# A scratch slot held longer, and the block sums of one weight chunk in eight moved from GpSimd to VectorE, in a two-layer encoder

## The chip, the cores and the metric

The kernel runs on one core of a Trainium2 chip. The metric is the device time of one execution in microseconds (us). A core has five engines that run side by side and wait for each other through semaphores: TensorE (PE, matmuls; PEld is its weight load), VectorE (DVE), ScalarE (ACT), GpSimd (POOL) and SyncE (SP, which here only issues DMAs). Each engine takes its own instructions strictly in order: one that waits holds up all that stand behind it on that engine.

## The reference, cut to what matters

A trunk of two pre-norm residual layers over 512 tokens of width 1024. Layer 0 mixes with two kinds of attention heads, layer 1 with a neighbourhood attention whose scores get a learned relative position bias. After each mixing step comes a squared-ReLU MLP of width 4096, and a norm ends the whole:

```python
def sq_relu_mlp(h, w_up, w_down):
    u = jax.nn.relu(h @ w_up)
    return (u * u) @ w_down
...
        h = h + sq_relu_mlp(rmsnorm(h, norm_ffn[layer]), ffn_w_up[layer], ffn_w_down[layer])
    return rmsnorm(h, final_norm)
```

Everything is float32. The bias of layer 1 is `rpb[:, rblk, cblk]`, looked up for each query and key in its window.

## The kernel before, in words

**Precision.** Every float32 operand of a matmul is split into a high half, rounded to the matmul's format (`F32R`), and a low half, the rest. ACT makes the high half by a copy, DVE (sometimes POOL) the low half by a subtraction. A product is three matmuls: high by high, high by low, low by high (`mm3`, L604 to L606; L448 to L450 for blocks of 256 columns).

**Memory.** Large tiles live in 32 slots of 128 x 1024 (`Slot`). `take` takes the first of the list `free`, `give` appends to its end, at the time the program is built. A new tile of a slot waits, on the chip, until the last reader of the slot's tile before is done. Weight chunks pass through `wp`: four `raw` buffers (loaded by SP), three `whi`, four `wlo`.

**Weights.** `plan` writes down which chunks will be needed, `weights(i)` brings chunk `i` up and looks ahead: up to five loads, two splits. Three kinds of chunk matter here. `chunk` loads and splits. `summed_chunk` (L245 to L260) lets ACT write `wlo` as the negated raw chunk (L255), then a DMA on POOL's queue adds the weights from memory onto it (L256), and ACT writes `whi` (L259). `seven_chunk` (L349 to L367) loads two blocks of 128 rows by 256 columns, forms the four further block sums by three POOL instructions (L356, L357, L358; 128, 256 and 128 wide), then has ACT write `whi` (L362) and DVE `wlo` (L363), seven blocks of 128 columns each.

**Seven blocks.** `Seven` multiplies 2 x 2 blocks with seven block products instead of eight. `sums` and `split` bring the other factor into seven blocks, each a high and a low half, in slots of its own (DVE L390, L393, L418, L422 and ACT L417 where `convert` does it). `run` multiplies: for each of its weight chunks 7 x 3 matmuls of 256 columns (L448 to L450), then ACT and DVE put the result together (L456 to L460).

**The MLP.** `mlp(l, last)` is called once per layer, `last` only in the second. Its second half goes like this. `product8` multiplies eight hidden tiles `U` by eight chunks of the down weights into all eight PSUM banks: the first two chunks interleaved, then chunk by chunk, and the last two (U6, U7) output column by output column, each column being added to the residual `hT` by DVE (L1536). Beside it `convert` turns the other hidden tiles, in pairs `R` (eight pairs in the first MLP, seven in the second), into the seven blocks, and in the first MLP `bias_rows` builds the bias tables of layer 1: it loads the bias in pieces into one slot (`R` there), POOL spreads it over another (`F`, L1481 to L1484), and SP writes 32 pieces of `F` to the DRAM tile `bx` (L1490, L1495). Then `F` is given back. During this part `reserve` forbids weight chunks to take slots. Next `u7.run` goes over four groups `m` of 256 output columns, with eight (seven) weight chunks in each; each group's result is added to `hT` (L1574). In the first group of the first MLP `beside` also splits the last pair `V` into two tiles `U4` (`split`: high half L964 on ACT, low half L961 on DVE), which a last plain product multiplies after the groups (`gens4`).

**Order.** A scheduler puts the instructions of each engine in order when the program is built. What is wrapped in `tc.keep_in_program_order` (`held`) keeps its place; so do the block sums on POOL.

Of the kernel before, what the change touches and what calls it, by code (L numbers as in the profile page):

```python
# [12 lines left out]
ALU = mybir.AluOpType  # L13
# [5 lines left out]
P = 128  # L19
# [11 lines left out]
def f32(ap):  # L31
    return ap.bitcast(F32)
# [3 lines left out]
def encoder_kernel(ctx: ExitStack, tc: tile.TileContext, ins, out, dbg=None):  # L36
    nc = tc.nc
    PE, ACT, DVE, POOL, SP = nc.tensor, nc.scalar, nc.vector, nc.gpsimd, nc.sync
# [22 lines left out]
    def nm(s):  # L61
        cnt[0] += 1
        return f"{s}_{cnt[0]}"
# [198 lines left out]
    def rows(w, k0, nk):  # L262
        return w[k0 * P : (k0 + nk) * P, :].rearrange("(k p) n -> p k n", p=P)
# [6 lines left out]
    def plan(*spec, make=None):  # L270
        asked.append((make or chunk, spec))
        return len(asked) - 1
# [71 lines left out]

    reserve = [3]

    def seven_chunk(w, k0, c0):


        slot = Slot(F32) if len(free) > reserve[0] else None  # L350
        raw = slot.t if slot else wp.tile([P, 1024], F32, tag="raw", bufs=4, name=nm("raw"))
        SP.dma_start(raw[:, 0:512].rearrange("p (k n) -> p k n", k=2), rows(w, k0, 2)[:, :, c0 : c0 + 256])
        r = raw.rearrange("p (b n) -> p b n", n=P)
        yield
        held = tc.keep_in_program_order
        held(POOL.tensor_tensor(r[:, 6], r[:, 0], r[:, 1], op=ALU.subtract))  # L356
        held(POOL.tensor_tensor(r[:, 4:6], r[:, 2:3].to_broadcast([P, 2, P]), r[:, 0:7:6], op=ALU.add))  # L357
        held(POOL.tensor_tensor(r[:, 7], r[:, 3], r[:, 5], op=ALU.subtract))  # L358
        yield
        hi = wp.tile([P, 1024], F32R, tag="whi", name=nm("whi"))  # L360
        lo = wp.tile([P, 1024], F32R, tag="wlo", bufs=4, name=nm("wlo"))
        ACT.activation(hi[:, 0:896], raw[:, 128:1024], AF.Copy)  # L362
        DVE.tensor_tensor(lo[:, 0:896], raw[:, 128:1024], f32(hi[:, 0:896]), op=ALU.subtract)  # L363
        if slot:
            slot.free()
        yield hi, lo, []

    class Seven:
# [29 lines left out]
        def split(self, kp, held=lambda z: z):  # L398

            for b in range(7):  # L400
                i = self.number(kp, b) // 2
                if i not in self.slots:
                    self.slots[i] = Slot()
            raw, t = self.raw.pop(kp)
            own = isinstance(t, Slot)
            r, t_ = (s_.rearrange("p (b n) -> p b n", n=256) for s_ in (raw.t, t.t if own else t))

            T4 = t_[:, 2:3] if own else r[:, 3:4]
            src = lambda b, n: (r[:, 1 + b : 1 + b + n] if b < 3 else t_[:, b - 3 : b - 3 + n] if b < 5
                                else r[:, 0:1] if b == 5 else T4)  # L410
            b = 0
            while b < 7:
                q = self.number(kp, b)
                n = 2 if b == 3 or (b < 2 and q % 2 == 0) or (b == 5 and not own) else 1
                d = self.slots[q // 2].t.rearrange("p (q z n) -> p q z n", q=2, z=2)[:, q % 2 : q % 2 + n]
                s_ = r[:, 0:4:3] if b == 5 and n == 2 else src(b, n)
                ACT.activation(d[:, :, 0], s_, AF.Copy)  # L417
                held(DVE.tensor_tensor(d[:, :, 1], s_, f32(d[:, :, 0]), op=ALU.subtract))  # L418
                b += n
                yield  # L420
                if b == 3 and not own:
                    held(DVE.tensor_tensor(r[:, 3], r[:, 3], r[:, 0], op=ALU.subtract))  # L422
                    yield
            raw.free()
            if own:
                t.free()
# [4 lines left out]

        def plan(self, w, c0, pairs=None):

            return [plan(w, pairs[kp] if pairs else 2 * kp, c0, make=seven_chunk) for kp in range(self.np)]

        def run(self, ids, evac):

# [129 lines left out]
    def tiles(c0, n):  # L567
        return [(c0 + o, min(P, n - o)) for o in range(0, n, P)]
# [219 lines left out]
    hold = {}  # L788
# [683 lines left out]
    def bias_rows():  # L1472

        R, F = Slot(F32), Slot(F32)
        Fi, Fe = F.t[:, 0:376], F.t[:, 376:1024]
        rpb = ins["od_rpb"][0]
        for qr in range(8):
            SP.dma_start(R.t[16 * qr : 16 * qr + 16, 0:248],
                           rpb.rearrange("h a b -> h (a b)")[:, (7 - qr) * 31 : (7 - qr) * 31 + 248])
            yield  # L1480
        POOL.memset(F.t, NEG)  # L1481
        rv = R.t[:, 0:248].rearrange("p (k d) -> p d k", d=31)
        POOL.tensor_copy(Fi.rearrange("p (j k) -> p j k", k=8)[:, 15:31, :], rv[:, 7:23, :])
        POOL.tensor_copy(Fe[:, 128:376].rearrange("p (j k) -> p j k", k=8), rv)  # L1484
        R.free()
        for _ in range(6):
            yield
        bxv = bx.rearrange("t (c r) h k -> t c (r h) k", r=8)
        for c in range(16):
            SP.dma_start(bxv[0, c], Fi[:, (15 - c) * 8 : (15 - c) * 8 + 256])  # L1490
            yield

            at, step = (0, 128 + (7 - c) * 8) if c < 8 else (128 + (23 - c) * 8, 248 - (23 - c) * 8)
            two = Fe[:, at : at + 2 * step].rearrange("p (z n) -> p z n", z=2)[:, :, 0:128]
            SP.dma_start(bxv[1, c].rearrange("q (z n) -> q z n", z=2), two)  # L1495
            yield
        F.free()
        yield

    def convert(u7, R):  # L1500
        held = tc.keep_in_program_order
        for kp, raw in enumerate(R):
            yield from u7.sums(kp, raw, DVE, held)
            yield
            yield from u7.split(kp, held)

    def mlp(l, last=None):

        stage, ahead, later = first_product(l)
        reserve[0] = 3
        w = ins["ffn_w_down"][l]
        up4, gens4 = [], []

        def plain_last(k0, V):
            left = list(V)
            gens4.extend(product(w, k0, up4, tiles(512 * c, 512), lambda j, b, c=c: ev(4 * c + j, b), nk=2 * len(V))
                         for c in range(2))  # L1520

            def beside(m, i):
                if m == 0 and i % 8 == 4 and left:
                    w_ = left.pop(0)
                    for z in range(2):
                        U4.append(Slot())
                        up4.append(U4[-1].pair())
                        split(w_.t[:, S * z : S * z + S], up4[-1])
                    w_.free()

            return beside

        U4 = []

        def ev(m, b):
            return DVE.tensor_tensor(hT[:, m, :], hT[:, m, :], b, op=ALU.add)  # L1536

        U, _, _, (at_u, _), _ = stage(SIZES[l][0])
        up = [s_.pair() for s_ in U]
        gens = [product(w, at_u, up, tiles(512 * c, 512), lambda j, b, c=c: ev(4 * c + j, b)) for c in range(2)]  # L1540
        ahead()
        for c, gen in enumerate(gens):
            for i, _ in enumerate(gen):
                later(c, i)
        for s_ in U:
            s_.free()
        U, R, V, (at_u, at_r), late = stage(*SIZES[l][1:])
        first = [k + z for k in at_u for z in range(2)]
        gen = product8(w, first, U, ev)
        u7 = Seven(2 * len(R))  # L1550
        ids = [u7.plan(w, 256 * m, at_r) for m in range(4)]
        k0 = 32 - 2 * len(V)
        beside = (last or plain_last)(k0, V)
        bias = iter(()) if last else bias_rows()
        reserve[0] = NSLOT
        work, at = convert(u7, R), 0
        for i, _ in enumerate(gen):
            if i in (1, 4, 6):
                next(late, None)
            next(bias, None)  # L1560

            at += 9 * len(R) + 2
            while at > 0:
                next(work, None)
                at -= 8 * len(U) - 2
        for x in (work, bias):
            for _ in x:
                pass
        reserve[0] = 3
        for m in range(4):  # L1570

            def evac(w_):
                h2 = hT[:, 2 * m : 2 * m + 2, :]
                DVE.tensor_tensor(h2, h2, w_.t.rearrange("p (z n) -> p z n", z=2), op=ALU.add)  # L1574

            for i, _ in enumerate(u7.run(ids[m], evac)):
                beside(m, i)
        u7.free()
        for gen in gens4:
            for _ in gen:  # L1580
                pass
        for s_ in U4:
            s_.free()

    mlp(0)


# [483 lines left out]
```

## Time and profile before

| | us |
|---|---|
| median of 3 runs | 1172.02 |
| lowest, highest | 1170.26, 1172.5 |
| the profiled execution | 1172.01 |
| its span in the trace | 1170.2 |
| mean granted clock of PE | 0.996 |

The span is the time from the first to the last instruction that the profile shows. Rows of a timeline have the start, the duration, the engine with line and operation, the tile written and read, and in brackets how long the engine had been idle and what released it. Rows of waits have who waited for whom, the total, how often, and the longest. A window's row has its borders, its length, the busy time of PE, PEld, DVE, ACT and POOL (with the number of instructions), the granted clock of PE (1.00 is full speed), the DMA engines' share and GB/s.

### The profile page before, as it was taken

The page shows a single profiled execution, that of the slowest core. Times are in us where ns is not written, and L with a number is a line of the kernel's source. Part 1 is how long each engine was busy: PE and PEld are TensorE (multiplying, and loading weights), DVE is VectorE, ACT ScalarE, POOL GpSimd, SP SyncE. Part 2 cuts the span into 40 slices and gives each one's busy share as a digit, 9 for nine tenths or more (in the row PEclk, how much of TensorE's full clock was granted, in tenths as well). Part 3 has the DMA queues.
Part 4 walks back from the last instruction along what each step waited for, and adds up shares of the span by engine and source line. Part 5 has one row for each costly group of instructions (what it writes and reads, how often), then busy time and mean ns, then how long its engine had stood idle before and what let it go on. Part 6 is the DMA issues. An engine that isn't in the chain of part 4 may idle for free.

```text
span 1170.2 us, 20549 instructions
## 1 busy us (share of the span) xinstructions
PE 1150.1 (98%) x7348; PEld 1025.0 (88%) x7348; DVE 892.2 (76%) x1544; ACT 668.5 (57%) x1135; POOL 602.9 (52%) x743
## 2 busy tenths in 40 slices
PE   9999999999999999899999999999999999999997
PEld 7787888888899998689987998988888999989996
DVE  6887988878868876676595676767997788688765
ACT  6676876756256658433453555655552665773445
POOL 4356252207688992359802232221287799426960
PEclk9999999999999999899999999999999999999999
DMA  7322414222523327623446565434343233282432
GB/s 233 108 75 66 96 59 132 64 82 88 173 76 88 100 73 219 181 82 99 127 127 158 136 175 134 126 102 136 99 148 105 84 104 93 63 200 62 127 118 73
DMA packets 115350, 134.37 MB, mean 115 GB/s; under 512 B 9795, under 2 KB 96752, under 8 KB 115248
## 3 DMA queue, kind: packets, MB, share of 16 engines
q1 hardware_dynamic: 110896, 120.09, 34.8%
q0 software_dynamic: 4032, 12.60, 5.4%
q8 instruction: 58, 0.95, 0.3%
q14 instruction: 44, 0.36, 0.1%
q10 hardware_dynamic: 320, 0.36, 0.1%
HBM read 110.61 MB, written 6.29 MB: 100 GB/s over the span
## 4 chain that ended last, share of the span: by engine, by line
PE 79%; DVE 6%; POOL 5%; DMA 4%; issue 3%; ACT 1%; SPq 1%; DVEq 0%; POOLq 0%; ACTq 0%
PE mm L604 8%; PE mm L605 8%; PE mm L606 8%; PE s L1128 3%; PE mm L450 3%; PE mm L448 3%; PE mm L449 3%; PE o L1116 3%; PE t L1103 2%; PE t L450 2%; PE t L448 2%; PE t L449 2%; PE s L606 2%; PE s L604 2%; PE s L605 2%
## 5 line engine op out<-in xcount | busy, mean ns | idle before, releaser
L604 PE MATMUL mm<-a,whi 128*128 128x512 f32 x428 | 174.0, 407 | 0.2
L363 DVE TENSOR_TENSOR wlo<-a,whi 128x896 fp32r<-128x896 f32 x103 | 129.6, 1261 | 54.7 <-ACT whi L362 54.4
L605 PE MATMUL mm<-a,whi 128*128 128x512 f32 x428 | 169.1, 395 | 0.0
L606 PE MATMUL mm<-a,wlo 128*128 128x512 f32 x428 | 169.1, 396 | 0.0
L362 ACT ACTIVATE whi<-a 128x896 fp32r<-128x896 f32 x103 | 97.7, 949 | 106.2 <-PE o L449 24.2
L233 ACT ACTIVATE whi<-raw 128x1024 fp32r<-128x1024 f32 (+3 forms) x100 | 92.2, 924 | 67.3 <-PE s L605 24.3
L223 DVE TENSOR_TENSOR wlo<-raw,whi 128x1024 fp32r<-128x1024 f32 (+4 forms) x97 | 110.1, 1140 | 25.2 <-ACT whi L233 25.0
L450 PE MATMUL mm<-a,wlo 128*128 128x256 f32 x430 | 120.7, 281 | 1.0 <-DVE wlo L363 1.0
L448 PE MATMUL mm<-a,whi 128*128 128x256 f32 x430 | 120.8, 281 | 0.0
L449 PE MATMUL mm<-a,whi 128*128 128x256 f32 x430 | 120.6, 280 | 0.0
L363 DVE TENSOR_TENSOR wlo<-raw,whi 128x896 fp32r<-128x896 f32 x61 | 72.3, 1190 | 50.2 <-ACT whi L362 49.9
L362 ACT ACTIVATE whi<-raw 128x896 fp32r<-128x896 f32 x61 | 57.9, 952 | 86.6 <-POOL raw L358 54.0
L358 POOL TENSOR_TENSOR a<-a 128x128 f32<-128x128 f32 x103 | 99.9, 970 | 8.1
L357 POOL TENSOR_TENSOR a<-a 128x256 f32<-128x256 f32 x103 | 93.8, 911 | 8.1
L606 PEld LDWEIGHTS mm<-a,wlo 128*128 128x128 f32 x428 | 80.4, 188 | 18.2
L604 PEld LDWEIGHTS mm<-a,whi 128*128 128x128 f32 x428 | 80.6, 188 | 17.3 <-issue 0.9
L605 PEld LDWEIGHTS mm<-a,whi 128*128 128x128 f32 x428 | 80.8, 189 | 14.8 <-DVE a L961 0.2
L1136 POOL TENSOR_SCALAR p<-p,ti 128x512 f32<-128x512 f32 x64 | 45.3, 708 | 86.3 <-DVE ti L1135 61.5
L1714 POOL TENSOR_SCALAR p<-p,ti 128x256 f32<-128x256 f32 x64 | 35.4, 563 | 105.2 <-DVE ti L1713 90.4
L448 PE MATMUL t<-a,whi 128*128 128x256 f32 x312 | 87.8, 281 | 0.0
L450 PE MATMUL t<-a,wlo 128*128 128x256 f32 x312 | 87.5, 281 | 0.0
L449 PE MATMUL t<-a,whi 128*128 128x256 f32 x312 | 87.5, 280 | 0.0
(429 smaller groups left out, 3595.5 us busy)
## 6 DMA issues: line engine op xcount, KB each, us to landing
a<-in_ffn_w_up_dram SPq DMA_DIRECT2D x102, 256.0 KB, 2.8
raw<-in_ffn_w_down_dram SPq DMA_DIRECT2D x34, 512.0 KB, 4.2
raw<-in_ffn_w_down_dram SPq DMA_DIRECT2D x59, 256.0 KB, 2.6
raw<-in_od_w_qkv_dram SPq DMA_DIRECT2D x64, 128.0 KB, 3.1
raw<-in_ffn_w_up_dram SPq DMA_DIRECT2D x12, 512.0 KB, 3.9
wlo<-in_ffn_w_down_dram POOLq DMA_DIRECT2D x12, 512.0 KB, 6.4
a<-a SPq DMA_DIRECT2D x18, 256.0 KB, 3.3
bx<-a SPq DMA_DIRECT2D x32, 128.0 KB, 6.2
```

The costliest lines, as they stand in the source:

```text
L223: z = lambda: (eng or DVE).tensor_tensor(to, src, f32(high), op=ALU.subtract)
L233: ACT.activation(hi[:, 0:m], raw[:, 0:m], AF.Copy)
L357: held(POOL.tensor_tensor(r[:, 4:6], r[:, 2:3].to_broadcast([P, 2, P]), r[:, 0:7:6], op=ALU.add))
L358: held(POOL.tensor_tensor(r[:, 7], r[:, 3], r[:, 5], op=ALU.subtract))
L362: ACT.activation(hi[:, 0:896], raw[:, 128:1024], AF.Copy)
L363: DVE.tensor_tensor(lo[:, 0:896], raw[:, 128:1024], f32(hi[:, 0:896]), op=ALU.subtract)
L448: PE.matmul(o, wh, x[:, 0], start=kp == 0 and n in (0, 1, 3, 5), stop=False, skip_group_check=True)
L449: PE.matmul(o, wh, x[:, 1], start=False, stop=False, skip_group_check=True)
L450: PE.matmul(o, wl, x[:, 0], start=False, stop=kp == self.np - 1, skip_group_check=True)
L604: PE.matmul(o, wh, xh, start=first, stop=False)
L605: PE.matmul(o, wh, xl, start=False, stop=False)
L606: PE.matmul(o, wl, xh, start=False, stop=last)
```

## The change

Two edits. `bias_rows` no longer gives the tables' slot `F` back when the last piece is issued; `mlp` gives it back after the seven-block product of the first MLP, behind `u7.free()`. And `seven_chunk` can be told an engine for its block sums: `Seven.plan` names VectorE for the fourth chunk (`kp == 3`) of each group wherever a list of row pairs is given, which is so in the second products of both MLPs and nowhere else. There the three sums are not held in program order but placed by the scheduler.

```diff
-    def seven_chunk(w, k0, c0):
+    def seven_chunk(w, k0, c0, eng=None):
...
-        held = tc.keep_in_program_order
-        held(POOL.tensor_tensor(r[:, 6], r[:, 0], r[:, 1], op=ALU.subtract))
-        held(POOL.tensor_tensor(r[:, 4:6], r[:, 2:3].to_broadcast([P, 2, P]), r[:, 0:7:6], op=ALU.add))
-        held(POOL.tensor_tensor(r[:, 7], r[:, 3], r[:, 5], op=ALU.subtract))
+        held = (lambda z: z) if eng else tc.keep_in_program_order
+        eng = eng or POOL
+        held(eng.tensor_tensor(r[:, 6], r[:, 0], r[:, 1], op=ALU.subtract))
+        held(eng.tensor_tensor(r[:, 4:6], r[:, 2:3].to_broadcast([P, 2, P]), r[:, 0:7:6], op=ALU.add))
+        held(eng.tensor_tensor(r[:, 7], r[:, 3], r[:, 5], op=ALU.subtract))
...
-            return [plan(w, pairs[kp] if pairs else 2 * kp, c0, make=seven_chunk) for kp in range(self.np)]
+            return [plan(w, pairs[kp] if pairs else 2 * kp, c0, DVE if pairs and kp == 3 else None, make=seven_chunk)
+                    for kp in range(self.np)]
...
-        F.free()
+        hold["tables"] = F
         yield
...
         u7.free()
+        if not last:
+            hold["tables"].free()
```

In the program that this gives, the order on PE and on SP is as before. POOL has 24 instructions fewer and DVE the same 24 more. In the first group of the first MLP the three sums stand on DVE among the last steps of `convert`, before the first `wlo` (L363) of the groups; in each later group they stand between the `wlo` of its first and of its second chunk; in the second MLP's first group they stand just before the first `wlo`. L964 and L961 move behind the conversion of the last two pairs.

## Prediction

> **What bounds the kernel now.** I read the page first, for which engine sets the end.
>
> ```profile
> span 1170.2 us, 20549 instructions
> PE 1150.1 (98%) x7348; PEld 1025.0 (88%) x7348; DVE 892.2 (76%) x1544; ACT 668.5 (57%) x1135; POOL 602.9 (52%) x743
> ```
>
> TensorE is busy for 98% of the span, so the kernel is a string of matmuls, and only gaps in that string can be won. The change touches the second product of the first MLP, so the windows of that stage come next (columns: window, length, busy time of each engine with its count, granted clock, DMA share, GB/s). 484.88 is where the last two chunks of the plain second product start on PE, 502.88 where the seven-block product starts, 587.04 where it ends.
>
> ```profile
> 440.00:484.88 44.88, 44.88 (x246) 38.68 (x244) 26.93 (x46) 30.67 (x47) 6.36 (x8) 1.00 0.83 225
> 484.88:502.88 18.00, 13.68 (x50) 10.32 (x49) 17.64 (x27) 7.51 (x12) 10.27 (x14) 0.81 0.40 103
> 502.88:508.16 5.28, 3.58 (x26) 3.02 (x24) 5.28 (x8) 3.22 (x4) 2.36 (x3) 1.00 0.02 3
> 508.16:574.80 66.64, 64.75 (x547) 64.14 (x546) 43.19 (x44) 24.66 (x28) 60.25 (x73) 1.00 0.34 103
> ```
>
> Up to 484.88 PE has no gap. It stands still for 4.3 us of the second window and 1.7 us of the third, and DVE (17.64 of 18.00, then 5.28 of 5.28) has no pause there. In the fourth POOL is the fullest engine (60.25 of 66.64). Who waits is in the view of waits from 470 to 512 us.
>
> ```profile
> ACT a L964 <- DMA bx<-a: 8.5, 1, 8.5
> DVE a L961 <- ACT a L964: 8.4, 1, 8.4
> PE s L604 <- ACT whi L259: 3.9, 1, 3.9
> ```
>
> One ACT instruction waits 8.5 us for the DMAs that write the bias tables, and DVE waits 8.4 us behind it. The timelines of ACT and DVE put this in order:
>
> ```profile
> 472.84 1.23 ACT L417 ACTIVATE a<-a 128x512 fp32r<-128x512 f32 x3
> 482.56 0.63 ACT L964 ACTIVATE a<-a 128x512 fp32r<-128x512 f32 x1 [8.49 <-DMA bx<-a]
> 484.57 1.04 ACT L255 ACTIVATE wlo<-raw 128x1024 fp32r<-128x1024 f32 x1
> 488.54 1.04 ACT L259 ACTIVATE whi<-raw 128x1024 fp32r<-128x1024 f32 x1
> 474.10 0.69 DVE L390 TENSOR_TENSOR sc<-a 128x512 f32<-128x512 f32 x1
> 483.22 0.69 DVE L961 TENSOR_TENSOR a<-a,a 128x512 fp32r<-128x512 f32 x1 [8.44 <-ACT a L964]
> 506.80 1.08 DVE L363 TENSOR_TENSOR wlo<-raw,whi 128x896 fp32r<-128x896 f32 x1
> ```
>
> L964 is the high half of the first `U4` tile. Slots are handed out first in, first out, and by the code this tile gets the slot that `bias_rows` has just given back, so it may not be written before the last table DMA has read it. Queued behind L964 on ACT stand the weights of the product's last chunk: its `wlo` start (L255, 484.57), which a POOL DMA then completes, and its `whi` (L259, 488.54). PE shows the price:
>
> ```profile
> 479.19 0.40 PE L606 MATMUL s<-a,wlo 128*128 128x512 f32 x1
> 485.34 0.40 PE L606 MATMUL s<-p,wlo 128*128 128x512 f32 x1
> 489.64 0.79 PE L604 MATMUL s<-p,whi 128*128 128x512 f32 x1 [3.90 <-ACT whi L259]
> 491.28 0.79 PE L606 MATMUL s<-p,wlo 128*128 128x512 f32 x1 [0.42 <-DMA wlo<-in_ffn_w_down_dram]
> 494.43 0.63 PE L604 MATMUL t<-p,whi 128*128 128x512 f32 x1
> 502.65 0.39 PE L606 MATMUL s<-p,wlo 128*128 128x512 f32 x1
> 505.74 0.39 PE L448 MATMUL o<-a,whi 128*128 128x256 f32 x1 [0.71 <-DVE hT L1536]
> 507.94 0.38 PE L450 MATMUL s<-a,wlo 128*128 128x256 f32 x1 [0.98 <-DVE wlo L363]
> 574.80 0.39 PE L450 MATMUL mm<-a,wlo 128*128 128x256 f32 x1 [1.01 <-DVE wlo L363]
> ```
>
> Beside the gaps, the matmuls after 489.64 take 0.63 us instead of 0.39 until past 494.43: that is the clock of 0.81. The 48 matmuls of the last two chunks last from 484.88 to 502.88, 18.0 us, where 0.23 us each (479.19 to 485.34 is 27 steps of 0.228) make 11.0. So 7.0 us are lost before the seven-block product starts, and about 2.3 us in its first two chunks (a 256-column matmul starts every 0.118 us, below, and chunk 1's third, 24th in all, should start 2.7 us after 502.88 instead of 5.06). With the 1.2 us at 574.80 this is 10.5 us; the whole stage, 484.88 to 587.04, holds 102.2 us against 11.0 + 672 x 0.1176 = 90.0 without any gap. **12.1 us is therefore all that the stage can give.**
>
> **The slot that is kept.** The tables' slot now stays taken, and the two `U4` tiles get the next slots in the list: those of the last two converted outputs. In the changed program L964 and L961 stand behind the conversion of these outputs on ACT and DVE, among waits that DVE itself fulfils. The 8.44 us of DVE waiting and the 8.49 of ACT go. What is late next? Of the last chunk's weights, `whi` has three buffers and waits for the matmuls of the fifth chunk, which end just after 479.19; with 1.04 for the copy it is there at about 480.7, before 485.6. `wlo` moves with L255 by 8.5, from 484.57 to 476.1, and so does its arrival, from 491.28 to 482.8; PE wants it at 485.8. Both are in time, with 3.0 us to spare for the slower one. One more wait appears: the fifth output's last tile gets the slot in which the raw bias was loaded. Before, the L964 wait covered it. Those loads are over long before 474, as POOL read that slot from 443.30 to 444.84 for the tables; only the table DMAs go on, the last one issued at 475.88:
>
> ```profile
> 443.30 1.54 POOL L1484 COPY a<-a 128x248 f32<-128x248 f32 x1
> 475.88 0.97 SPq L1495 DMA_DIRECT2D bx<-a  x1
> ```
>
> The new wait costs nothing. So DVE becomes the bound of the join: it works from 474.79 to the second block chunk's `wlo` (L363, 506.80) without a pause except the 8.44, and PE needs that `wlo` at 484.88 + 11.0 + 2.7 = 498.6. The first term is the shift of this DVE chain, **-8.4 us**: PE passes that point at about 499.5 instead of 507.94. It will still wait about 1 us there, and the gap of 0.71 at 505.74 is swallowed by it, since the evacuations move with the chain.
>
> **The block sums on DVE.** Each moved chunk is three DVE instructions, 128, 256 and 128 wide, in place of three on POOL; four chunks in each MLP, 24 instructions in all. DMAs do not change and SP's order stays. DVE's rows for this form are:
>
> ```profile
> 470.40 0.42 DVE L393 TENSOR_TENSOR a<-a,sc 128x256 f32<-128x256 f32 x1
> 562.44 1.19 POOL L358 TENSOR_TENSOR raw<-raw 128x128 f32<-128x128 f32 x1
> 555.66 0.46 POOL L358 TENSOR_TENSOR raw<-raw 128x128 f32<-128x128 f32 x1
> ```
>
> 0.69 for 512 (L390) and 0.42 for 256 leave 0.29 for 128 on the same line, an estimate; three make 1.0 us, at most 1.26 (all at the 256 price) and not under 0.42. Group 0's three stand inside the DVE chain above, before its `wlo` instructions, so they cost **+1.0 us**. Against that, POOL and DVE slow each other (L358 takes 1.19 beside a DVE L363 and 0.46 alone), and POOL has three chunks instead of four beside this chain. I take 0.4 us back; 0 to 0.8 is possible, by how much DVE's L390, L393 and L418 were stretched there. The Trainium skill (GPSIMD Engine Reference, Specifications) says that GpSimd's SBUF interface is shared with VectorE and contends with DVE instructions that have two SBUF inputs, as these sums are. By that rule the relief of POOL below shrinks by the sums' own length, from 2.6 to 1.6 us a group; the pair 1.19 and 0.46 agrees with it.
>
> Further on the sums relieve POOL. Its groups and PE's chunks:
>
> ```profile
> 552.74 1.30 POOL L356 TENSOR_TENSOR raw<-raw 128x128 f32<-128x128 f32 x1
> 573.76 1.30 POOL L356 TENSOR_TENSOR raw<-raw 128x128 f32<-128x128 f32 x1
> 570.23 0.28 PE L448 MATMUL s<-a,whi 128*128 128x256 f32 x1
> 572.70 0.28 PE L448 MATMUL s<-a,whi 128*128 128x256 f32 x1
> ```
>
> POOL needs 21.0 us for eight chunks, PE 8 x 2.47 = 19.8. POOL loses 1.2 us a group on PE until its lead is gone at 574.80. With seven chunks it needs 18.4, or 19.4 with the sums' blocking, so PE leads no more, and the gap of 1.01 us with its slow matmul goes: **-1.2 us** (0 if the lead after the join is short). In the later groups the three sums cost DVE 1.0 us of its slack: 43.19 busy of 66.64.
>
> **The second MLP** has the sums but no slot change. There PE has no gap in the seven-block product:
>
> ```profile
> 1067.40:1137.00 69.60, 69.60 (x594) 69.60 (x593) 46.85 (x47) 30.01 (x36) 55.57 (x66) 1.00 0.39 122
> 1067.07 0.28 PE L448 MATMUL s<-a,whi 128*128 128x256 f32 x1
> 1067.40 1.09 DVE L363 TENSOR_TENSOR wlo<-raw,whi 128x896 fp32r<-128x896 f32 x1 [0.43 <-ACT whi L362]
> ```
>
> Nothing is to be won. The second chunk's `wlo` ends at 1068.5. The product's first matmul starts at 1067.1, so it asks for that `wlo` 2.7 us later, at 1069.8; a delay of 1.0 fits into 1.3. I take 0, up to +1.
>
> **The sum:** -8.4 + 1.0 - 0.4 - 1.2 = -9.0 us. What follows (the rest of the MLP, layer 1) waits for PE or for loads that move with it, so the shift reaches the end. The profiled execution took 1172.01 us, with a span of 1170.2; the median of the runs is 1172.02, so no correction is needed: **1163.0 us**.
>
> **The rivals.**
> (a) *The weights' DMAs take ACT's place.* The bias tables' DMAs run on till 482.5, and the last chunk's `wlo` would now be loaded beside them. For it: a DMA share of 0.83 up to 484.88, and table DMAs that land late, in the view of the `bx` tile from 440 to 500; the second row is for (c):
>
> ```profile
> DMA to landing us min/median/max: 2.0/6.1/10.9
> raw<-in_ffn_w_down_dram SPq DMA_DIRECT2D x59, 256.0 KB, 2.6
> ```
>
> If the accumulating DMA took 10.9 us from about 478.0 (L255's end plus its issue), PE would go on at 488.9 instead of 491.28, with the slow stretch kept: 2.4 us won there, 2 more where DVE no longer holds chunk 1, 1.2 at the end, less the 1.0: 4.6, so 1167.4. By the Trainium skill (TensorE: Matmul & The Clock Gate, Part 1) the clock halves after about 3.4 us of idling; a gap of 3.1 us might escape it, and the time would be near 1165. Against (a): 3.0 us to spare. 0.15.
> (b) *The change does not do what it says:* some other slot makes ACT wait to 482.5 all the same, or the chain is held there by another. Then +1.0 and -1.2 remain, 1171.8. Against it: the new tenant's only foreign wait is for loads that had landed by 443.3. 0.08.
> (c) *DVE waits for loads (slower).* At each of six later group starts (three in each MLP) a sum on DVE waits for its raw load, which is issued only once an L363 shortly before has freed the buffer; DVE's later `wlo` and the evacuations are queued behind it. With no lead left, each costs the load's 2.6 us and 1.0 for the sums: 21.6 us in all, 1184.6. It decides from 1.5 us at each start (9.0 over six). Against it: one chunk of PE, 2.47 us, lies between, and DVE idles a third of that stage. 0.05.
>
> **How the numbers follow.** The forecast has 0.62, its own range 1160 to 1166: the 12.1 us limit on one side (1159.9), on the other sums at 1.26, nothing back from POOL, no 1.2, +1 in the second MLP (-8.4 + 1.3 + 1.0 = -6.1). Cases between it and (a) have 0.10, (a) 0.15, (b) 0.08, (c) 0.05. The range 1160.0 to 1167.5 reaches to (a) and leaves out (b) and (c). 0.2% is 2.3 us, about what a measurement of this kernel can tell from no change: faster 0.87, same 0.08, slower 0.05.
>
> **What would show it.** Right: ACT L964 without a wait for `bx`; ACT and DVE with no idle stretch of over 2 us between 474 and 490; PE with no gap at the last chunk and a clock of 1.00 there, the seven-block product starting near 496, one gap of about 1 us in its second chunk for DVE's `wlo`, none at its fourth group; the first MLP over 9 us sooner, the second unchanged. Wrong: ACT waiting for another DMA before 482, PE waiting for `wlo` or `raw` DMAs, DVE's L356 waiting for loads, or new gaps at group starts of the second MLP.

## The result

The changed kernel takes 1162.51 us (median of 4 runs, 1161.59 to 1163.99) where the kernel before took 1172.26 (4 runs): the ratio is 0.9917, 95% interval 0.9894 to 0.9939. In a second set of runs it was 1162.36 us and 0.9918 (0.9905 to 0.9931). It is faster by 9.6 to 9.8 us; the forecast was 9.0.

The page of the changed kernel, its span and TensorE's share (PE lost 3.8 us of busy time, most of it matmuls that had run at the low clock, and 5.2 us of standing still):

```profile
span 1161.2 us, 20538 instructions
PE 1146.3 (99%) x7348; PEld 1022.4 (88%) x7348; DVE 901.3 (78%) x1568; ACT 669.2 (58%) x1135; POOL 586.4 (51%) x719
```

The windows of the changed kernel. The first two are cut at the same points of the program as those shown of before; the third ends at the second block chunk's third matmul, the fourth just behind the end of the stage (window, length, busy us with count of PE, PEld, DVE, ACT and POOL, granted clock, DMA share, GB/s):

```profile
440.00:484.70 44.70, 44.70 (x244) 38.51 (x242) 35.14 (x59) 34.85 (x52) 10.59 (x14) 1.00 0.93 248
484.70:495.58 10.88, 10.88 (x50) 9.01 (x48) 10.60 (x19) 3.39 (x6) 4.67 (x8) 1.00 0.23 73
495.58:498.95 3.37, 2.89 (x24) 2.68 (x22) 3.37 (x6) 3.07 (x4) 0.24 (x1) 1.00 0.02 5
498.95:577.00 78.05, 77.68 (x653) 77.13 (x654) 56.50 (x61) 30.68 (x36) 62.07 (x72) 1.00 0.39 121
```

The last two chunks of the plain product take 10.88 us instead of 18.00, with the clock at 1.00 instead of 0.81. VectorE works 35.14 us of the first window instead of 26.93: that is work which stood behind the wait for the tables before. In the timelines of ACT and DVE the wait for `bx` is gone; L966 (L964 before) now waits 0.89 us for VectorE, and stands behind the last chunk's `wlo` (L255) and the conversion:

```profile
461.18 1.06 ACT L255 ACTIVATE wlo<-raw 128x1024 fp32r<-128x1024 f32 x1 [0.35 <-DMA raw<-in_ffn_w_down_dram]
475.24 1.06 ACT L255 ACTIVATE wlo<-raw 128x1024 fp32r<-128x1024 f32 x1 [0.58 <-DMA raw<-in_ffn_w_down_dram]
488.63 0.63 ACT L966 ACTIVATE a<-a 128x512 fp32r<-128x512 f32 x1 [0.89 <-DVE a L419]
481.44 1.22 DVE L391 TENSOR_TENSOR sc<-a 128x512 f32<-128x512 f32 x1
485.30 0.60 DVE L357 TENSOR_TENSOR raw<-raw 128x128 f32<-128x128 f32 x1 [0.28 <-DMA raw<-in_ffn_w_down_dram]
497.82 1.08 DVE L364 TENSOR_TENSOR wlo<-raw,whi 128x896 fp32r<-128x896 f32 x1
```

TensorE's gaps in the stage are two small ones, and one of 1.13 us has come in a place that the change does not touch, the second MLP's first product, where the kernel before had none:

```profile
498.95 0.39 PE L452 MATMUL s<-a,wlo 128*128 128x256 f32 x1 [0.48 <-DVE wlo L364]
524.56 0.39 PE L452 MATMUL mm<-a,wlo 128*128 128x256 f32 x1 [0.33 <-DVE wlo L364]
576.28 0.39 PE L606 MATMUL s<-a,whi 128*128 128x512 f32 x1
958.87 0.38 PE L452 MATMUL s<-a,wlo 128*128 128x256 f32 x1 [1.13 <-DVE wlo L364]
```

The third of these rows is the first matmul after the stage, which was at 587.04: the stage ends 10.8 us sooner, and 1.8 us of that are lost again until the end, of which this gap is 1.13.

### The profile page after: what moved, and what is told of

It is laid out like the page before. It is cut to its first block, busy times and chain, and to the rows that moved or that the text cites. A ratio compares the mean times of both kernels' runs of the same rounds, so it can differ in the third digit from the quotient of the medians.

```text
span 1161.2 us, 20538 instructions
## 1 busy us (share of the span) xinstructions
PE 1146.3 (99%) x7348; PEld 1022.4 (88%) x7348; DVE 901.3 (78%) x1568; ACT 669.2 (58%) x1135; POOL 586.4 (51%) x719
## 4 chain that ended last, share of the span: by engine, by line
PE 87%; DVE 5%; DMA 2%; issue 2%; ACT 1%; POOL 1%; SPq 0%; DVEq 0%; ACTq 0%; POOLq 0%
PE mm L606 8%; PE mm L607 8%; PE mm L608 8%; PE mm L452 4%; PE mm L450 4%; PE mm L451 4%; PE s L1130 3%; PE o L1118 3%; PE t L450 3%; PE t L452 3%; PE t L451 3%; PE s L608 2%; PE s L606 2%; PE s L607 2%; PE t L1105 2%
## 5 line engine op out<-in xcount | busy, mean ns | idle before, releaser
L364 DVE TENSOR_TENSOR wlo<-a,whi 128x896 fp32r<-128x896 f32 x103 | 130.7, 1272 | 55.3 <-ACT whi L363 54.9
L363 ACT ACTIVATE whi<-a 128x896 fp32r<-128x896 f32 x103 | 97.6, 948 | 105.0 <-PE o L607 27.6
L363 ACT ACTIVATE whi<-raw 128x896 fp32r<-128x896 f32 x61 | 57.9, 952 | 80.5 <-POOL raw L359 37.9
L364 DVE TENSOR_TENSOR wlo<-raw,whi 128x896 fp32r<-128x896 f32 x61 | 73.2, 1214 | 36.0 <-ACT whi L363 36.0
L358 POOL TENSOR_TENSOR a<-a 128x256 f32<-128x256 f32 x103 | 93.7, 910 | 8.1
```

The source lines that it names most:

```text
L358: held(eng.tensor_tensor(r[:, 4:6], r[:, 2:3].to_broadcast([P, 2, P]), r[:, 0:7:6], op=ALU.add))
```

## The experiments

Theory A: the gain is the tenant of the tables' slot, and the sums on VectorE add little. Its rivals: the two parts need each other; the sums are worth much more, or cost; holding the slot does something else. The table has each kernel's time, its ratio to the kernel before on the same chip (whose medians there were 1171.13, 1171.23 and 1170.68 us), and three points of one profiled execution on TensorE: the third matmul of the second block chunk (507.94 before, 498.95 after), the first matmul behind the seven-block stage of the first MLP (587.04, 576.28), and the first one behind that of the second MLP (1138.08, 1128.88).

| kernel | us (runs) | ratio, 95% interval | chunk 2 | stage end | second MLP |
|---|---|---|---|---|---|
| before, as above | 1172.26 (4) | | 507.94 | 587.04 | 1138.08 |
| before_again | 1170.66 (1) | | 506.66 | 585.76 | 1136.67 |
| changed, as above | 1162.51 (4) | 0.9917 (0.9894 to 0.9939) | 498.95 | 576.28 | 1128.88 |
| after_again | 1162.36 (5) | 0.9918 (0.9905 to 0.9931) | 499.88 | 577.78 | 1129.79 |
| e1_slot_only | 1163.57 (5) | 0.9943 (0.9930 to 0.9955) | 499.94 | 579.23 | 1129.42 |
| e4_other_tenant | 1164.46 (5) | 0.9939 (0.9925 to 0.9953) | 499.78 | 579.11 | 1130.69 |
| e2_sums_only | 1169.78 (11) | 0.9989 (0.9980 to 0.9998) | 506.24 | 583.51 | 1135.76 |
| e3_sums_first_mlp | 1161.68 (4) | 0.9922 (0.9908 to 0.9935) | 498.89 | 576.17 | 1128.15 |
| e5_sums_later_groups | 1162.54 (5) | 0.9932 (0.9920 to 0.9944) | 500.32 | 577.89 | 1129.44 |
| e6_two_chunks | 1161.24 (4) | 0.9912 (0.9898 to 0.9926) | 499.65 | 576.50 | 1128.45 |
| e7_tables_later | 1161.19 (4) | 0.9911 (0.9897 to 0.9925) | 498.47 | 576.67 | 1127.36 |
| e8_tables_two | 1162.20 (5) | 0.9924 (0.9912 to 0.9937) | 499.40 | 577.95 | 1128.81 |
| e9_third_too | 1166.77 (5) | 0.9962 (0.9949 to 0.9976) | 503.18 | 580.15 | 1132.56 |

### The slot alone, and the sums alone

The slot alone (all sums on GpSimd):

```diff
-            return [plan(w, pairs[kp] if pairs else 2 * kp, c0, DVE if pairs and kp == 3 else None, make=seven_chunk)
+            return [plan(w, pairs[kp] if pairs else 2 * kp, c0, None, make=seven_chunk)
```

> The slot is kept as in the change, but all block sums stay on GpSimd. Theory A (the gain is the tenant of the slot; the sums on VectorE are worth only the 1.2 us of GpSimd's late gap): VectorE's chain ahead of the second block chunk is 1.0 us shorter, TensorE passes that chunk without the gap of 0.48 us, the seven-block stage starts near 495.6, and the late gap of 1 to 2 us for GpSimd stays: 1163 to 1164 us, 0 to 1.5 above the changed kernel. Theory B (the two parts need each other): TensorE enters the stage 7 us sooner than GpSimd had planned for, GpSimd's 21.0 us for eight chunks against TensorE's 19.8 has less lead to live on, and 3 to 5 us are given back as gaps for the halves of the block chunks: 1166 to 1168 us.

The sums alone:

```diff
-        hold["tables"] = F
+        F.free()
...
-        if not last:
-            hold["tables"].free()
```

> The slot is given back as before the change; the fourth chunk of each group is summed on VectorE in both MLPs. Theory A: the wait of ScalarE's L966 for the table DMAs, 8 us, is there as before, TensorE's gap of 3.9 us and the slow clock too; the sums cost up to 1.0 in the first group and take away the gaps of 0.8 and 1.0 us before the third and fourth group: 1171 to 1172.5 us, no difference to the kernel before. Rival (relief of GpSimd brings a good part of the gain): 1165 to 1169 us.

Measured: 0.9943 for the slot, some 6.7 us, and 0.9989 for the sums, 1.3 us (0.2 to 2.3). Together they make 8.0 where the change has 9.6 to 9.8. The intervals reach over a microsecond to either side, so the runs show no gain that only both parts together give. Theory B of the first expectation, 3 to 5 us given back, falls; but what theory A said of the second chunk did not come either, for TensorE stands still there for 1.39 us. In the view of waits of the sums-only kernel (470 to 512 us) and on its TensorE the old wait stands as it was:

```profile
ACT a L966 <- DMA bx<-a: 8.6, 1, 8.6
DVE a L963 <- ACT a L966: 8.6, 1, 8.6
```

```profile
488.49 0.50 PE L606 MATMUL s<-p,whi 128*128 128x512 f32 x1 [3.23 <-ACT whi L259]
```

At the stage's end the slot alone is worth 7.8 us, the sums alone 3.5, both 10.8 (each 1.3 less against before_again, below). So the sums are worth more there than the forecast had. The slot-only kernel's TensorE shows one reason, the late gap for GpSimd's sums (567.00), and its VectorE the other: the chain from L391 to the second chunk's L364, which the forecast lengthened by the sums, is no shorter without them.

```profile
499.94 0.38 PE L452 MATMUL s<-a,wlo 128*128 128x256 f32 x1 [1.39 <-DVE wlo L364]
567.00 0.38 PE L452 MATMUL mm<-a,wlo 128*128 128x256 f32 x1 [1.00 <-DVE wlo L364]
482.20 1.22 DVE L391 TENSOR_TENSOR sc<-a 128x512 f32<-128x512 f32 x1
498.81 1.08 DVE L364 TENSOR_TENSOR wlo<-raw,whi 128x896 fp32r<-128x896 f32 x1
```

498.81 - 482.20 = 16.61 us without sums; 497.82 - 481.44 = 16.38 us with three (the rows of the change, above). The two kernels that give the slot back early say the same: from this L390 (L391) to the second chunk's `wlo` VectorE takes 13.98 us before (from 492.82, to the L363 at 506.80 that the prediction shows) and 13.45 with the sums alone:

```profile
492.82 1.22 DVE L390 TENSOR_TENSOR sc<-a 128x512 f32<-128x512 f32 x1
491.66 1.22 DVE L391 TENSOR_TENSOR sc<-a 128x512 f32<-128x512 f32 x1
505.11 1.08 DVE L364 TENSOR_TENSOR wlo<-raw,whi 128x896 fp32r<-128x896 f32 x1
```

In these two, one of the `U4` low halves (0.60 us) stands ahead of the stretch and not in it. GpSimd works 6.1 us beside it before, 3.6 with the sums alone.

### Is it the tenant?

The slot is given back early, but put at the end of the list before the `U4` tiles are taken; sums on GpSimd as in the slot-only kernel:

```diff
-        hold["tables"] = F
+        F.free()
+        hold["tables"] = F.i
...
                     w_ = left.pop(0)
+                    if hold["tables"] in free:
+                        free.remove(hold["tables"])
+                        free.append(hold["tables"])
```

> All block sums on GpSimd, and the tables' slot is given back early as before the change; but it is moved to the end of the list of free slots, so that the two U4 tiles take slots 7 and 29 as they do in the slot-only kernel. Theory A (the loss came from the tenant of that slot, not from giving it back): no wait of ScalarE's L966 for the table DMAs, and the same time as the slot alone, 1163.6 us, within 1. Rival (holding the slot does something else, such as taking a slot from the raw weights of the block chunks): 1165 us or more, toward the 1171 of before.

Measured: 0.9939 beside 0.9943, and the second chunk at 499.78 beside 499.94. The `U4` tiles had slots 7 and 29 in both. Theory A holds: what counts is that `U4` does not follow the tables into their slot. With the sums on GpSimd this kernel, too, has late gaps, and at both places where the kernel before had them:

```profile
545.87 0.39 PE L452 MATMUL s<-a,wlo 128*128 128x256 f32 x1 [1.00 <-DVE wlo L364]
566.89 0.39 PE L452 MATMUL mm<-a,wlo 128*128 128x256 f32 x1 [1.00 <-DVE wlo L364]
```

### Which of the sums count

Sums on VectorE in the first MLP alone:

```diff
-        def plan(self, w, c0, pairs=None):
+        def plan(self, w, c0, pairs=None, on=False):
...
-            return [plan(w, pairs[kp] if pairs else 2 * kp, c0, DVE if pairs and kp == 3 else None, make=seven_chunk)
+            return [plan(w, pairs[kp] if pairs else 2 * kp, c0, DVE if on and kp == 3 else None, make=seven_chunk)
...
-        ids = [u7.plan(w, 256 * m, at_r) for m in range(4)]
+        ids = [u7.plan(w, 256 * m, at_r, not last) for m in range(4)]
```

> The change with the sums on VectorE in the first MLP alone; the second MLP has all of them on GpSimd. Theory A: the second MLP's stage had no gap before and has none now, so 1162.5 us, within 1 of the changed kernel; and the gap of 1.13 us that the changed kernel has in the second MLP's first product lies before the sums in time, so it is there here too if it comes from the earlier shift of the engines against each other. Rival 1 (VectorE's sums in the second MLP cost their 1.0 us a group somewhere): 1159 to 1161.5 us. Rival 2 (they help GpSimd there): 1164 us or more.

The same edit with `m > 0` in place of `not last`:

> The change, but the sums go to VectorE only in groups 1 to 3 of each MLP; the first group's fourth chunk stays on GpSimd. Theory A: the first group's sums stand in VectorE's chain ahead of the second block chunk, 1.6 us in the profile (0.60, 0.68, 0.28); without them TensorE's gap of 0.48 us there goes and nothing else changes: 0.5 us sooner, 1162.0 us. Rival (GpSimd lacks the time that this chunk cost it): a gap of 1 us or more for GpSimd's sums in groups 0 or 1, 1163.5 us or more.

And a second chunk of each group (`kp in (3, 6)`):

> The change with a second chunk of each group, the seventh, summed on VectorE as well. Theory A (GpSimd's lead is restored by the fourth chunk alone: the changed kernel has no gap in TensorE after 525 us of this stage): within 1 us of the change, 1162 to 1163.5. Rival 1 (each chunk moved takes away contention between GpSimd and VectorE, as it did in group 0): 1 us or more sooner, 1161.5 or less. Rival 2 (VectorE waits for the raw loads, or its three sums delay the evacuation that the next group needs): 1164 us or more, with gaps at group starts.

Measured: 0.9922, 0.9932 and 0.9912, whose intervals all overlap that of the change. The second MLP's sums do nothing that can be told, as forecast. The expectation for the first group was wrong: without its sums the second chunk came at 500.32, not sooner than in the two executions of the change (498.95 and 499.88), and the chain was 16.62 us, from 482.57 to 499.19, as in the slot-only kernel. A second chunk per group brings the stage's end 0.5 us forward against the mean of the two executions of the change (577.03), and those two differ by 1.5. Its 1161.24 us lies where its rival 1 had it, but the intervals do not tell it from the change.

### One more chunk on VectorE ahead of the join

```diff
-            return [plan(w, pairs[kp] if pairs else 2 * kp, c0, DVE if pairs and kp == 3 else None, make=seven_chunk)
+            return [plan(w, pairs[kp] if pairs else 2 * kp, c0, DVE if pairs and kp in (2, 3) else None, make=seven_chunk)
```

> The change with the third chunk of each group summed on VectorE too, so that in the first group six sums in place of three stand in VectorE's chain ahead of the second block chunk. That chain, from the start of VectorE's L391 (481.44 in the changed kernel) to the start of the second chunk's L364 (497.82), is 16.38 us with three sums and 16.61 with none. Theory A (each sum moved off GpSimd gives back its own length and more, because GpSimd slows VectorE by about as much while it works): 16.0 to 16.4 us, and 1161 to 1162.5 in all. Theory B (the sums cost their own 1.0 us less 0.4, as forecast; the three-sum figure is then owed to something else): 17.0 us or more, TensorE's gap there 0.6 longer, 1163 or more.

Measured: 1166.77 us, 4.3 to 4.4 more than the change by the medians and about 5.2 by the ratios, and by neither theory. VectorE's and GpSimd's timelines show the wait that the prediction had as its rival (c), in another place, the first group:

```profile
485.24 0.29 DVE L357 TENSOR_TENSOR raw<-raw 128x128 f32<-128x128 f32 x1 [6.44 <-DMA raw<-in_ffn_w_down_dram]
488.20 0.68 DVE L391 TENSOR_TENSOR sc<-a 128x512 f32<-128x512 f32 x1
488.81 0.68 DVE L419 TENSOR_TENSOR a<-a,a 128x512 fp32r<-128x512 f32 x1
489.41 0.42 DVE L394 TENSOR_TENSOR a<-a,sc 128x256 f32<-128x256 f32 x1
490.68 0.28 DVE L357 TENSOR_TENSOR raw<-raw 128x128 f32<-128x128 f32 x1
490.88 0.42 DVE L423 TENSOR_TENSOR a<-a 128x256 f32<-128x256 f32 x1
502.05 1.08 DVE L364 TENSOR_TENSOR wlo<-raw,whi 128x896 fp32r<-128x896 f32 x1
497.72 0.65 POOL L357 TENSOR_TENSOR raw<-raw 128x128 f32<-128x128 f32 x1 [13.21 <-DMA raw<-in_ffn_w_down_dram]
```

The third chunk's sum came to VectorE 6.44 us before its weights were there. But GpSimd, too, stood idle here until 497.72, and so the kernel measured the disputed thing by accident: what VectorE's chain costs with almost nobody beside it (GpSimd works 2.2 of these 13.85 us, at the end). From L391 at 488.20 to L364 at 502.05 are 13.85 us, of which 0.60 (488.81 to 489.41) belong to an L419 that stood ahead of L391 in the change: 13.25 us for the work that took 16.38 in the change, 0.28 of it the wait of L357 for its load.

Single instructions say the same. Both L391 of this stretch take 0.68 us here. In the change the first takes 1.22, beside GpSimd's sums (481.44, above), and the second 0.68, while GpSimd stands still; in the slot-only kernel the second takes 0.94. These are the second L391 of the change and of the slot-only kernel, and the latter's window:

```profile
488.52 0.68 DVE L391 TENSOR_TENSOR sc<-a 128x512 f32<-128x512 f32 x1
488.31 0.94 DVE L391 TENSOR_TENSOR sc<-a 128x512 f32<-128x512 f32 x1
488.31:489.20 0.89, 0.89 (x6) 0.73 (x5) 0.89 (x3) 0.64 (x1) 0.89 (x2) 1.00 0.00 0
```

In that window GpSimd is busy throughout and the DMA engines move nothing, so it is not the transfers that slow VectorE there.

Three undisturbed sums hold VectorE for 0.20 + 0.33 + 0.20 = 0.73 us from start to next start (the first is 490.68 to 490.88), not for 1.0, the sum of their durations. So the slot-only chain would be 13.25 - 0.73 = 12.52 us alone; it was 16.61, a loss of 4.1 beside 3.1 in the change (2.85 without the wait for the load). One chunk more on GpSimd costs VectorE 1.0 to 1.2 us here, more than the chunk's own 0.73.

### The tables' DMAs later, and both edits

In the change VectorE's chain begins with waits of ACT's L255 for raw weight loads that run beside the table DMAs (0.35 and 0.58 us, above). Here the table DMAs go out beside every fourth step of the groups:

```diff
+        held = tc.keep_in_program_order
...
-            SP.dma_start(bxv[0, c], Fi[:, (15 - c) * 8 : (15 - c) * 8 + 256])
+            held(SP.dma_start(bxv[0, c], Fi[:, (15 - c) * 8 : (15 - c) * 8 + 256]))
...
-            SP.dma_start(bxv[1, c].rearrange("q (z n) -> q z n", z=2), two)
+            held(SP.dma_start(bxv[1, c].rearrange("q (z n) -> q z n", z=2), two))
...
-            next(bias, None)
+            if not last and i < 14:
+                next(bias)
...
-        for x in (work, bias):
-            for _ in x:
-                pass
+        for _ in work:
+            pass
...
                 beside(m, i)
+                if i % 4 == 2:
+                    next(bias, None)
+        for _ in bias:
+            pass
```

> The change with the 32 table DMAs moved behind: one beside every fourth step of the seven-block groups instead of from 445 to 476 us. Theory A (the chain that ends at the second block chunk begins with ScalarE's L255, which waits at 461 us for a raw weight load that runs beside the table DMAs, 0.35 us in the changed kernel and 1.50 with the slot alone): that wait goes, VectorE's chain starts up to 1.5 us sooner, TensorE's gap at the second chunk falls from 0.5 to 0.9 us to nothing: 1161.5 to 1162 us. Rival (the table DMAs only move their harm: the raw loads of the block chunks land later, GpSimd and VectorE wait for them, and TensorE has new gaps in the groups): 1164 us or more.

The same with the chunks 4 and 7 on VectorE:

> Both edits that came out best together: the table DMAs beside the seven-block groups, and the fourth and the seventh chunk of each group summed on VectorE. Theory A (they act on different waits: the first takes the wait of L255 at 461 us out of VectorE's chain, the second frees GpSimd in the groups, where the first left two gaps of 0.48 and 0.78 us): the gaps add up and go, 1159.5 to 1160.5 us. Rival (both gains are the same microsecond, the arrival at the second chunk): 1161.2 us, as each alone.

Measured: 0.9911 and 0.9924. Of the first, half of each theory came true. L255 waits no more, and TensorE passes the second chunk without a gap. VectorE's chain does not start sooner, though: its L391 comes at 482.93, later than in the change, and it is the chain that is shorter, 14.06 us, because GpSimd has done its sums by 484.5 and stands still until 492.68:

```profile
482.93 1.23 DVE L391 TENSOR_TENSOR sc<-a 128x512 f32<-128x512 f32 x1
496.99 1.08 DVE L364 TENSOR_TENSOR wlo<-raw,whi 128x896 fp32r<-128x896 f32 x1
```

Then two gaps come later (0.48 us at 523.85 and 0.78 at 544.64); a second chunk off GpSimd did not remove them (0.64 and 0.96 us in the second kernel), so the gains did not add up. The second kernel's timelines of GpSimd and VectorE ahead of its gap at 545.97 show why: GpSimd now waits for raw loads at the group's end, works later, and stretches the L364 that is queued behind the evacuation's 1024-wide L1577.

```profile
542.28 0.46 POOL L357 TENSOR_TENSOR raw<-raw 128x128 f32<-128x128 f32 x1 [1.15 <-DMA raw<-in_ffn_w_down_dram]
543.65 1.32 POOL L359 TENSOR_TENSOR raw<-raw 128x128 f32<-128x128 f32 x1
543.24 1.42 DVE L1577 TENSOR_TENSOR hT<-hT,a 128x1024 f32<-128x1024 f32 x1
544.58 1.34 DVE L364 TENSOR_TENSOR wlo<-raw,whi 128x896 fp32r<-128x896 f32 x1
```

No kernel here beats the change by more than the intervals leave open; the two best stand 0.06% under it.

### The same kernels once more

> The changed kernel itself once more. If the gap in the second MLP's first product (1.13 us at 958.87) belongs to the order and timing of the engines there, it comes back at 0.5 to 1.2 us; if it was chance of one execution, it is not there and the time is about 1161.5. The wait of ScalarE's L255 at 461 us for a raw load says how far the start of VectorE's chain differs from one execution to the next: 0.35 us again if it follows from the schedule, 1 to 2 if it is chance. Time 1162.5, within 1.

> The kernel before once more, for what one execution differs from the next. If the second MLP's first product has no gap there because nothing has shifted, it has none again; if the gap is chance, one of 0.2 to 1.1 us shows near 968 us. The wait of ScalarE's L255 near 463 us for a raw load was 2.00 us and may differ by 1; the end of the stage is set by the table DMAs' landing all the same, so the stage ends at 587, within 0.5.

Measured: the second execution of the change has a longer gap at the second chunk, and then the low clock, in the rows of its TensorE, ACT and windows:

```profile
499.88 0.38 PE L452 MATMUL s<-a,wlo 128*128 128x256 f32 x1 [1.39 <-DVE wlo L364]
461.64 1.06 ACT L255 ACTIVATE wlo<-raw 128x1024 fp32r<-128x1024 f32 x1 [1.30 <-DMA raw<-in_ffn_w_down_dram]
464.44 1.06 ACT L255 ACTIVATE wlo<-raw 128x1024 fp32r<-128x1024 f32 x1 [0.70 <-DMA raw<-in_ffn_w_down_dram]
476.22 1.06 ACT L255 ACTIVATE wlo<-raw 128x1024 fp32r<-128x1024 f32 x1 [0.85 <-DMA raw<-in_ffn_w_down_dram]
498.50:505.00 6.50, 5.12 (x30) 5.12 (x31) 5.25 (x8) 2.07 (x3) 2.24 (x3) 0.74 0.27 85
```

ACT's L255 waited 0.93 us in all in the first execution and 2.85 in this one (the sum of the three rows), and VectorE's chain starts at 482.37 instead of 481.44 with the same 16.38 us to go. So the 0.5 us gap of the first profile was luck; 1.39 us is what six of the profiles have. The kernel before has the stage's end at 585.76 this time: ACT's wait for `bx` is as long (8.46 us), but it begins and ends 1.2 us earlier. My 587 within 0.5 was too narrow. The gap of 1.13 us in the second MLP's first product is there again in the change, and absent again in the kernel before.

## Why the prediction was right, and where it was not

**The wait for the tables** went as forecast: no wait for `bx`, the last chunk's weights in time, no gap and no slow clock ahead of the seven-block product, which starts at 495.58 ("near 496"). The forecast of the next limit was right too: VectorE's chain sets the second chunk, forecast for 499.5 (500.1 with the sums), measured 498.95 and 499.88, with a gap of "about 1 us" that was 0.48 and 1.39. The wait itself was priced rightly: 8.49 us, and 8.46 in the second execution of the kernel before. But the slot is worth less than its wait. Against the two executions of before (507.94, 506.66) the kernels with the slot alone (499.94, 499.78) pass the second chunk 6.7 to 8.2 us sooner. Part of the spread is only when VectorE came to the L390 (L391) ahead of the wait: 474.10 and 472.87 in the two executions of before, 473.11 and 472.58 with the slot alone. With that taken out it is 6.6 to 7.0 us, and their ratios give 6.7 and 7.1. The forecast had moved VectorE's chain as it was, but it changed on the way: with the slot alone VectorE waits 1.4 and 1.8 us for an L418 of ScalarE, where it had no such wait before, and the stretch ahead of the second chunk takes 16.61 us in place of 13.98, 0.60 of it for the other `U4` low half; GpSimd works 11.1 us beside it, where it worked 6.1 before.

**The block sums ahead of the join** were the step that failed, in sign: forecast +1.0 for themselves and -0.4 for less contention, together +0.6; measured 16.38 against 16.61 us, -0.2, and without the slot 13.45 against 13.98, -0.5. The sums hold VectorE for 0.73 us, and GpSimd's chunk had cost it 1.0 to 1.2. The rows of before showed the contention (L390 in the chain takes 0.94 and 1.22 us where it takes 0.69 alone), but I sized the relief by a small share of it. The page of the Trainium skill that I named (GPSIMD Engine Reference, Specifications) has the contention of GpSimd's SBUF interface with VectorE; I used it for the relief of GpSimd alone, and the runs show VectorE slowed too: one L391 takes 0.68 us alone, 0.94 and 1.22 beside GpSimd.

**GpSimd's late gaps** were worth more than the 1.2 us of the forecast. From the second chunk to the stage's end TensorE takes 79.1 us before (in both executions) and 77.3 with the sums alone: 1.8 us. It takes 79.3 in both kernels with the slot alone, and 77.3, 77.3 and 77.9 in the change, e3 and after_again: 1.4 to 2.0 us. The sum had only the gap at 574.80; the kernel before has another of 0.82 us at 553.77, which I had not priced. Ahead of both, ScalarE's L362 waits 1.69 us for GpSimd's L358, and the sums-only kernel has neither gap. (GpSimd was not the fullest engine of that window, as I had called it: TensorE has 64.75 us there, GpSimd 60.25.)

**The second MLP** was forecast at 0, and that holds for the sums there (0.9922 without them, 0.9918 with). What I had not: between the two stages, where "what follows" was to move along, 1.0 to 1.7 us were lost. The gap near 959 us is 1.13, 1.13, 0.95, 0.81, 0.95, 0.94 us in the kernels with sums on VectorE and the slot kept, 0.73 with the sums alone, 0.32 and 0.22 with the slot alone, 0.36 and 0.29 with the tables later, none in the two executions of before. The sums-only kernel has the same instructions in the same order on every engine from the end of the first stage to there as the kernel before, so neither the order nor the kept slot is needed for the gap; how the engines stand to one another in time is what is left. Nothing here tests that, and what would set it, I have not found.

**The rivals.** (a), the weights' DMAs in ACT's place, did not come: TensorE has no gap at the last chunk. Its remark that a gap of 3.1 us might escape the low clock has a case against it: the second execution of the kernel before has a gap of 3.15 us in the last chunk, and its granted clock is 0.50 from 490.25 to 493.67. (b) falls with the slot's tenant. (c), a sum on VectorE that waits for its load, was a real danger and stood close: in the change the fourth chunk's sums wait 0.28 us in the first group, and in the first MLP 0.50 at most in the first execution, 1.20 in the second; in e9 the third chunk's wait 6.44, and that kernel is 4 to 5 us slower than the change. It struck in the first group and not at the later group starts where I had put it.

So the total came out within 0.8 us by luck, because errors cancelled: the slot is worth about 7 us and not 8.4, the sums 1 to 3 us (1.3 alone, 2.9 as the difference of 0.9943 and 0.9918) and not 0.6 (the 1.2 of GpSimd's gap less the 0.6 ahead of the join).

## What to carry to other kernels

Before keeping or freeing a buffer, look whose reads the next tenant inherits: a tile that takes a slot from a long train of DMA reads puts its whole engine queue behind the last of them. When work is moved from GpSimd to VectorE, price it by VectorE's time with and without GpSimd beside it, and not by the moved instructions alone; here the moved work paid for itself. Move only work whose inputs are there when the in-order queue reaches it: one chunk earlier lost 4 to 5 us, more than all the sums had gained.

## What the runs showed of the hardware that I had not expected

The low clock can follow a short gap, and does not always. In the slot-only kernel and in after_again the gap of 1.39 us is followed, 0.6 and 0.3 us after its end, by a stretch of 3.41 us in which the granted clock is 0.50 and the matmuls come every 0.21 us instead of 0.118. These are the first and the last matmul of fifteen in the slot-only kernel's stretch and one behind it, and the windows ahead of the stretch, of it and behind it:

```profile
500.51 0.40 PE L450 MATMUL t<-a,whi 128*128 128x256 f32 x1
503.48 0.41 PE L452 MATMUL o<-a,wlo 128*128 128x256 f32 x1
504.16 0.28 PE L450 MATMUL t<-a,whi 128*128 128x256 f32 x1
497.11:500.52 3.41, 2.02 (x14) 1.65 (x14) 3.41 (x6) 2.56 (x4) 0.00 (x0) 1.00 0.00 0
500.52:503.93 3.41, 3.41 (x19) 3.41 (x18) 3.16 (x4) 0.16 (x1) 1.28 (x1) 0.50 0.28 83
503.93:507.34 3.41, 3.41 (x31) 3.41 (x31) 1.09 (x1) 1.73 (x2) 3.17 (x5) 1.00 0.53 169
```

Fifteen matmuls by 0.095 us more are 1.4 us lost there, as much as the gap itself. At the stage's end little of it is left: the slot-only kernel comes there at 579.23, the other-tenant kernel, without such a stretch but with one late gap for GpSimd more, at 579.11; and after_again takes 77.9 us from the second chunk to there where the first execution of the change took 77.3. In four other kernels (other tenant, later groups, two chunks, third too) the same gap of 1.39 us had no such stretch; this window of the other-tenant kernel has the clock at 1.00:

```profile
498.50:505.00 6.50, 5.16 (x41) 4.96 (x42) 6.03 (x8) 1.97 (x3) 2.42 (x2) 1.00 0.27 87
```

The Trainium skill (TensorE: Matmul & The Clock Gate, Part 1) has the clock set by a free-running window of about 3.4 us and lowered after at least one idle window. The lengths agree with such a window: 3.41 us here, and 6.83 in the kernel before (488.15 to 494.98). That TensorE was busy for 2.02 of the 3.41 us ahead of the stretch does not agree with a whole idle window. Why the same gap lowered the clock in two executions out of six, no run here shows.
